# A transformer layer at its two stage boundaries: the squares for the second normalisation written to a PSUM bank, in four pieces

## The chip, the core and the metric

The kernel runs on one core of one Trainium2 chip. A core has a matrix engine (TensorE, PE in the profile, with its weight loads shown apart as PEld), a vector engine (VectorE, DVE), a scalar engine (ScalarE, ACT), a small general engine (GpSimd, POOL) and an engine that issues most of the transfers (SyncE, SP). They run side by side and wait for each other through semaphores. Data lies in SBUF; the matrix engine writes its results to PSUM, a second memory of eight banks, each 512 fp32 numbers wide on all 128 partitions. The metric is the device time of one execution in microseconds (us).

## What is computed

One layer over 256 tokens of width D = 2048, in fp32: a gated feed-forward block, a token mixer (attention and an mLSTM) and a second feed-forward block. Between the blocks stands the piece that the change touches: the residual sum goes through a layer norm with learned gain and bias, and its result through a second layer norm, without parameters, whose output is scaled and shifted by vectors made from the condition `c`.

```python
def _modulate(x, shift, scale):
    return _layernorm(x) * (1 + scale) + shift

def _layer(...):
    h = _swiglu(_modulate(x, sh1, sc1), ffn1_w_in, ffn1_w_out)
    x = _layernorm(ALPHA * x + 0.5 * (1 + g1) * h, ln1_g, ln1_b)
    h = _token_mixer(_modulate(x, sh2, sc2), w_in, ...)
    x = _layernorm(ALPHA * x + (1 + g2) * h, ln2_g, ln2_b)
    h = _swiglu(_modulate(x, sh3, sc3), ffn2_w_in, ffn2_w_out)
    return _layernorm(ALPHA * x + 0.5 * (1 + g3) * h, ln3_g, ln3_b)
```

## The kernel before

Every fp32 product is made of three matmuls on rounded parts (`mm3`, lines 368 to 370: high times high, high times low, low times high). Weights arrive in 1 MB pieces (`raw`), ACT rounds each to its high part (line 142) and DVE takes the difference as the low part (line 143). Beside this stream DVE builds the conditioning vectors (`acc`, line 157, from `ar`). The 256 tokens are two halves of 128, called a = 0 and a = 1 below; `res` holds both.

`out_proj` ends a block: its last 512 columns are multiplied for a = 0 and then for a = 1 (`products(0)`, `products(1)`), into one PSUM tile each (`o_f` after the first feed-forward block, `o_mx` after the mixer). Then `boundary` runs, once after the first feed-forward block (at 769 us of the trace, the **first boundary**) and once after the mixer (at 1173 us, the **second boundary**). For each half it

- adds the product to the residual and takes its statistics (`add_up`, lines 432 to 437; `row_std`, 258 to 260, with the power on POOL at line 248 in `rsqrt`);
- runs the layer norm over `res` in two passes (`ln_affine`): line 485 subtracts the mean and multiplies by the gain, line 490 scales, adds the bias and gives the row sum of each piece (pieces of 1024, 512 and 512 columns);
- has ACT square each piece after a shift (line 495), of which only the row sum is used. The squares themselves are never read: they go to an SBUF tile `sq` in the pool `np2` or `np3`;
- makes mean and reciprocal deviation of the second normalisation from these sums in a row of DVE operations on single columns (`ln_stats`, lines 501 to 518);
- normalises 256 columns at a time (`n`: the first tile on DVE at line 310, the others on ACT at 312), transposes them on PE (`tp`, line 316), scales and shifts (`xf`, ACT 326 and DVE 323), and splits the result in high and low part (`xhi`, 332; `xlo`, 333).

PE takes up the first tiles of the next stage directly from `xf`, in single fp32 matmuls against the first three weight pieces (`cols_1024`, line 618: `mo` at the first boundary, `ge` at the second): all of a = 0, then all of a = 1.

The order on DVE inside `boundary` is the order of the code (`manual_schedule`); on the other engines a scheduler sets it. SBUF pools lie on a stack at the two ends of the memory: a tile of a new pool may lie where a pool just released had tiles, and its first writer then waits for their last reader. At the second boundary `np3` takes the room of `mx`, the mixer's pool, of which the tiles `yh` and `yl` are read by products of `products(1)`. PSUM has a pool of five banks for accumulators (`mm_tile`), given out in the order in which they come free, and one of three for the rest (`aux_tile`).

## Time and profile before

| | us |
|---|---|
| median of three runs | 1939.93 |
| lowest and highest of them | 1935.54, 1943.65 |
| the profiled execution | 1937.79 |
| its span in the trace | 1936.1 |
| PE busy in the span | 1895.1 |
| DVE busy | 1474.7 |
| ACT busy | 944.7 |

The profiled execution took 1937.79 us, of which the trace covers 1936.1; the other 1.7 lie around it. Times in the rows below count from the start of the span. A row of the timeline gives the start, the duration, the engine, the line, the operation with its output and inputs, and in brackets how long the engine had been idle and who ended that. The granted clock (PEclk) is the share of its full clock that TensorE was given.

### The profile page before, as it was taken

To read this page: it belongs to the slowest core of one execution; us is meant where nothing else is said; L and a number is where in the kernel's file an instruction comes from. 1 tells how busy PE (TensorE), PEld (TensorE's weight loads), DVE (VectorE), ACT (ScalarE), POOL (GpSimd) and SP (SyncE) were. 2 spreads that over 40 slices of the span, in tenths; PEclk is the share of its full clock that TensorE was granted. 3 is DMA by queue.
4 is the path that set the end of the run, shared out by engine and by line. 5 is a ranking of instruction groups with operands and counts; after the bars stand their busy time and mean duration, and the time that the engine had idled before them with its cause. 6 is when DMAs were issued, how large, how long until landed. Compare 5 with 4: busy or idle time off the path is not lost.

```text
span 1936.1 us, 32201 instructions
## 1 busy us (share of the span) xinstructions
PE 1895.1 (98%) x13069; PEld 1717.0 (89%) x13069; DVE 1474.7 (76%) x1818; ACT 944.7 (49%) x1336; POOL 56.4 (3%) x82
## 2 busy tenths in 40 slices
PE   6999999999999999999999999999999999999997
PEld 3999999999978887699999785998999999988886
DVE  6788988776889898688988787767766665555776
ACT  3554454443454554745755534555444444444552
POOL 1111100000000000000000000000000000000000
PEclk9999999999999999999999999999999999999999
DMA  9978869899898886499889783987776775655552
GB/s 357 378 261 313 324 229 310 299 315 303 278 343 304 284 302 219 142 317 305 291 293 306 276 298 140 309 294 251 253 253 226 261 238 196 239 184 188 194 195 87
DMA packets 295693, 510.90 MB, mean 264 GB/s; under 512 B 10834, under 2 KB 158706, under 8 KB 294520
## 3 DMA queue, kind: packets, MB, share of 16 engines
q1 hardware_dynamic: 287768, 480.53, 72.8%
q0 software_dynamic: 7776, 28.32, 4.1%
q8 instruction: 102, 1.67, 0.3%
q14 instruction: 47, 0.39, 0.1%
HBM read 506.71 MB, written 2.10 MB: 263 GB/s over the span
## 4 chain that ended last, share of the span: by engine, by line
PE 75%; issue 11%; DMA 6%; DVE 5%; ACT 2%; POOL 0%; SPq 0%; DVEq 0%; ACTq 0%; POOLq 0%
PE gu_f L369 8%; PE gu_f L370 8%; PE gu_f L368 8%; PE o_f L368 7%; PE o_f L370 7%; PE o_f L369 7%; PE s L369 5%; PE s L368 5%; PE s L370 5%; DMA ar<-in_w_ada_dram 3%; PE fh L368 2%; PE fh L370 2%; PE fh L369 1%; PE fs L370 1%; PE fs L369 1%
## 5 line engine op out<-in xcount | busy, mean ns | idle before, releaser
L157 DVE SCALAR_TENSOR_TENSOR acc<-ar,csil,acc 128x1024 f32<-128x1024 f32 x242 | 307.8, 1272 | 84.4 <-DMA ar<-in_w_ada_dram 83.2
L369 PE MATMUL s<-xlo_f,hi_s 128*128 128x256 f32 x768 | 213.4, 278 | 1.6 <-DVE xlo_f L300 1.6
L368 PE MATMUL s<-xhi_f,hi_s 128*128 128x256 f32 x768 | 213.4, 279 | 0.0
L370 PE MATMUL s<-xhi_f,lo_s 128*128 128x256 f32 x768 | 213.2, 278 | 0.0
L370 PE MATMUL gu_f<-xhi_f,lo_f2i 128*128 128x256 f32 x768 | 212.0, 276 | 0.0
L368 PE MATMUL gu_f<-xhi_f,hi_f2i 128*128 128x256 f32 x768 | 212.0, 276 | 0.0
L369 PE MATMUL gu_f<-xlo_f,hi_f2i 128*128 128x256 f32 x768 | 212.0, 276 | 0.0
L143 DVE TENSOR_TENSOR lo_f2i<-raw_f2i,hi_f2i 128x1024 fp32r<-128x1024 f32 x96 | 117.6, 1225 | 89.2 <-ACT hi_f2i L142 89.2
L370 PE MATMUL gu_f<-xhi_f,lo_f1i 128*128 128x256 f32 x640 | 176.7, 276 | 0.0
L368 PE MATMUL gu_f<-xhi_f,hi_f1i 128*128 128x256 f32 x640 | 176.7, 276 | 0.0
L369 PE MATMUL gu_f<-xlo_f,hi_f1i 128*128 128x256 f32 x640 | 176.7, 276 | 0.0
L142 ACT CAST hi_f2i<-raw_f2i 128x1024 fp32r<-128x1024 f32 x96 | 100.8, 1050 | 135.2 <-PE gu_f L369 124.3
L142 ACT CAST hi_s<-raw_s 128x1024 fp32r<-128x1024 f32 x96 | 100.4, 1051 | 130.4 <-PE s L369 87.5
L369 PEld LDWEIGHTS s<-xlo_f,hi_s 128*128 128x128 f32 x768 | 145.3, 189 | 1.9 <-DVE xlo_f L300 1.9
L370 PEld LDWEIGHTS s<-xhi_f,lo_s 128*128 128x128 f32 x768 | 145.2, 189 | 0.0
L368 PEld LDWEIGHTS s<-xhi_f,hi_s 128*128 128x128 f32 x768 | 145.0, 189 | 0.0
L368 PEld LDWEIGHTS gu_f<-xhi_f,hi_f2i 128*128 128x128 f32 x768 | 144.2, 188 | 0.2
L369 PEld LDWEIGHTS gu_f<-xlo_f,hi_f2i 128*128 128x128 f32 x768 | 144.2, 188 | 0.2
L370 PEld LDWEIGHTS gu_f<-xhi_f,lo_f2i 128*128 128x128 f32 x768 | 144.2, 188 | 0.0
L143 DVE TENSOR_TENSOR lo_f2o<-raw_f2o,hi_f2o 128x1024 fp32r<-128x1024 f32 x88 | 107.7, 1224 | 44.9 <-ACT hi_f2o L142 44.8
L143 DVE TENSOR_TENSOR lo_s<-raw_s,hi_s 128x1024 fp32r<-128x1024 f32 x96 | 115.9, 1221 | 29.6 <-ACT hi_s L142 29.5
L368 PE MATMUL o_f<-hi_f2o,hh 128*128 128x512 f32 x344 | 135.2, 393 | 0.0
(485 smaller groups left out, 5344.9 us busy)
## 6 DMA issues: line engine op xcount, KB each, us to landing
ar<-in_w_ada_dram SPq DMA_DIRECT2D x227, 512.0 KB, 5.3
raw_f2i<-in_ffn_w_in_dram SPq DMA_DIRECT2D x48, 1024.0 KB, 5.1
raw_s<-in_ffn_w_in_dram SPq DMA_DIRECT2D x47, 1024.0 KB, 7.7
raw_f1o<-in_ffn_w_out_dram SPq DMA_DIRECT2D x44, 1024.0 KB, 7.3
raw_f2o<-in_ffn_w_out_dram SPq DMA_DIRECT2D x44, 1024.0 KB, 5.1
raw_f1i<-in_ffn_w_in_dram SPq DMA_DIRECT2D x40, 1024.0 KB, 7.5
ar<-in_w_ada_dram POOLq DMA_DIRECT2D x48, 512.0 KB, 6.9
raw_mxo<-in_w_out_dram SPq DMA_DIRECT2D x16, 1024.0 KB, 6.7
```

The source lines that it names most:

```text
L142: S.copy(hi, src)
L143: return V.tensor_tensor(out=lo, in0=src, in1=hi.bitcast(F32), op=ALU.subtract)
L157: V.scalar_tensor_tensor(out=acc, in0=raw, scalar=csil[:, k:k + 1], in1=acc, op0=ALU.mult, op1=ALU.add)
L368: PE.matmul(o, ah, bh, start=start, stop=False)
L369: PE.matmul(o, ah, bl, start=False, stop=False)
L370: PE.matmul(o, al, bh, start=False, stop=stop)
```

## The change

The tile `sq` of SBUF goes. Each boundary takes one accumulator bank of PSUM (`mm_tile`) for the squares of both halves, all pieces on top of each other. A bank is 512 numbers wide, so the second pass of the layer norm and the squares are cut into four pieces of 512 columns instead of 1024, 512, 512. The shift of the squares is the mean of the first piece, now of 512 columns (factor -4/D for -2/D), and `ln_stats` is adapted: one more row sum to add to the mean, one more sum of squares (a DVE operation more, ahead of the first `yield 1`), and the difference of mean and shift is taken from the mean itself. In `boundary` the DVE order stays: the first of the pieces of a = 1 stands where it stood, the rest where the last two stood.

```diff
-        for i, (c0, c1) in enumerate(((0, 1024), (1024, 1536), (1536, 2048))):
-            r = res[:, a, c0:c1]
-            V.scalar_tensor_tensor(out=r, in0=r, scalar=rs, in1=lgb[1][:, c0:c1], op0=ALU.mult, op1=ALU.add,
-                                   accum_out=sums[:, i:i + 1])
+        for i in range(4):
+            cs = slice(i * 512, (i + 1) * 512)
+            r = res[:, a, cs]
+            total, squares = ((k, k + 1) for k in ((0, 1, 2, 6)[i], (5, 7, 8, 9)[i]))
+            V.scalar_tensor_tensor(out=r, in0=r, scalar=rs, in1=lgb[1][:, cs], op0=ALU.mult, op1=ALU.add,
+                                   accum_out=sums[:, slice(*total)])
             if i == 0:
-                V.tensor_scalar_mul(sums[:, 4:5], sums[:, 0:1], -2.0 / D)
-            sq = npool.tile([P, 1024], F32, tag="sq", name=f"sq_{tag}{a}{i}")
-            S.activation(sq[:, :c1 - c0], r, AF.Square, bias=sums[:, 4:5], accum_out=sums[:, 7 + i:8 + i])
+                V.tensor_scalar_mul(sums[:, 4:5], sums[:, 0:1], -4.0 / D)
+            S.activation(sq, r, AF.Square, bias=sums[:, 4:5], accum_out=sums[:, slice(*squares)])
             yield
 
     def ln_stats(out_, sums):
         s = [sums[:, i:i + 1] for i in range(10)]
-        V.tensor_tensor(out=s[1], in0=s[1], in1=s[2], op=ALU.add)
+        V.tensor_scalar(out=s[1], in0=s[1], scalar1=s[2], scalar2=s[6], op0=ALU.add, op1=ALU.add)
...
-        V.tensor_scalar(out=s[3], in0=s[1], scalar1=s[0], scalar2=1.0 / D, op0=ALU.subtract, op1=ALU.mult)
+        V.tensor_tensor(out=s[3], in0=mean, in1=s[4], op=ALU.subtract)
         yield
         V.tensor_scalar(out=s[2], in0=s[3], scalar1=s[3], scalar2=-1.0, op0=ALU.mult, op1=ALU.mult)
         yield
         V.tensor_scalar_add(s[2], s[2], EPS)
+        yield
+        V.tensor_tensor(out=s[7], in0=s[7], in1=s[5], op=ALU.add)
         yield 1
...
+        sq = mm_tile(f"sq_{tag}")
         with tc.manual_schedule(engines={mybir.EngineType.DVE}):
...
-            aff = [ln_affine(a, rs[a], mv[a], lgb, sums[a], tag) for a in range(2)]
+            aff = [ln_affine(a, rs[a], mv[a], lgb, sums[a], sq) for a in range(2)]
...
             next(aff[1])
             next(m0[2])
-            next(aff[1])
-            next(aff[1])
+            for _ in aff[1]:
+                pass
             together(lns[1])
```

On ACT, at the second boundary, for a = 0 (`hi_mxo` is the last weight piece of the mixer's projection; the brackets name the engines whose semaphores the instruction waits for). Before:

```order
L142 COPY hi_mxo_01_12275<-raw_mxo_0_12269 128x1024 [waits PE_49,Activation_49]
L495 ACTIVATE sq_12416,sums_12399<-res,sums_12399 128x1024 [waits DVE_49,PE_49,Pool_49]
L495 ACTIVATE sq_12419,sums_12399<-res,sums_12399 128x512 [waits DVE_49,Activation_49]
L495 ACTIVATE sq_12422,sums_12399<-res,sums_12399 128x512 [waits DVE_49,Activation_49]
L312 ACTIVATE n_12439<-res,mr_12401 128x256 [waits DVE_49,Pool_49]
L326 ACTIVATE xf_12451<-tp_12435,scsh 128x128 [waits PE_49]
```

And with the change:

```order
L142 COPY hi_mxo_01_12276<-raw_mxo_0_12270 128x1024 [waits PE_49,Activation_49]
L496 ACTIVATE sq_12404,sums_12400<-res,sums_12400 128x512 [waits DVE_49]
L496 ACTIVATE sq_12404,sums_12400<-res,sums_12400 128x512 [waits DVE_49,Activation_49] x3
L312 ACTIVATE n_12441<-res,mr_12402 128x256 [waits DVE_49,PE_49,Pool_49]
L326 ACTIVATE xf_12453<-tp_12437,scsh 128x128 [waits PE_49]
```

The first square no longer waits for PE; the wait for PE, which belongs to the memory that `np3` takes over, has moved on to the first writers of `n`.

On DVE, at the second boundary, the second pass and the statistics of a = 1 (`mr` holds what `ln_stats` gives). Before:

```order
L490 TENSOR_SCALAR res,sums_12400<-res,rs_12398,lb_11668 128x1024
L493 TENSOR_SCALAR sums_12400<-sums_12400 128x1
L490 TENSOR_SCALAR res,sums_12400<-res,rs_12398,lb_11668 128x512 x2
L501 TENSOR_TENSOR sums_12400<-sums_12400 128x1
L504 TENSOR_SCALAR mr_12402<-sums_12400 128x1
L506 TENSOR_SCALAR sums_12400<-sums_12400 128x1
L508 TENSOR_SCALAR sums_12400<-sums_12400 128x1
L510 TENSOR_SCALAR sums_12400<-sums_12400 128x1
L333 TENSOR_TENSOR xlo_f_12385<-xf_12451,xhi_f_12384 128x2x128
L333 TENSOR_TENSOR xlo_f_12385<-xf_12461,xhi_f_12384 128x2x128
L512 TENSOR_SCALAR sums_12400<-sums_12400 128x1
```

And with the change:

```order
L492 TENSOR_SCALAR res,sums_12401<-res,rs_12399,lb_11669 128x512
L495 TENSOR_SCALAR sums_12401<-sums_12401 128x1
L492 TENSOR_SCALAR res,sums_12401<-res,rs_12399,lb_11669 128x512 x3
L502 TENSOR_SCALAR sums_12401<-sums_12401 128x1
L505 TENSOR_SCALAR mr_12403<-sums_12401 128x1
L507 TENSOR_TENSOR sums_12401<-mr_12403,sums_12401 128x1
L509 TENSOR_SCALAR sums_12401<-sums_12401 128x1
L511 TENSOR_SCALAR sums_12401<-sums_12401 128x1
L513 TENSOR_TENSOR sums_12401<-sums_12401 128x1
L333 TENSOR_TENSOR xlo_f_12386<-xf_12453,xhi_f_12385 128x2x128
L333 TENSOR_TENSOR xlo_f_12386<-xf_12463,xhi_f_12385 128x2x128
L515 TENSOR_SCALAR sums_12401<-sums_12401 128x1
```

The sum of the first two squares (line 513) is new and stands ahead of the two `xlo` differences, so that the rest of the statistics of a = 1 (from line 512 before, 515 now) comes behind one operation more.

On PE, at the second boundary, where the matmuls of a = 0 (`ge_12561`, with the change `ge_12563`) end and the transposes of a = 1 begin. Before:

```order
L618 MATMUL ge_12561<-raw_gu_12392,xf_12468 128x512
L618 MATMUL ge_12560<-raw_gu_12392,xf_12468 128x512
L316 MATMUL tp_12493<-ident,n_12491 128x128 x2
L316 MATMUL tp_12498<-ident,n_12496 128x128 x2
L618 MATMUL ge_12561<-raw_gu_12392,xf_12468 128x512
L316 MATMUL tp_12506<-ident,n_12504 128x128 x2
L618 MATMUL ge_12562<-raw_gu_12386,xf_12501 128x512
L316 MATMUL tp_12517<-ident,n_12515 128x128 x2
L618 MATMUL ge_12563<-raw_gu_12386,xf_12501 128x512
L316 MATMUL tp_12522<-ident,n_12520 128x128 x2
```

And with the change:

```order
L622 MATMUL ge_12562<-raw_gu_12393,xf_12469 128x512
L622 MATMUL ge_12563<-raw_gu_12393,xf_12469 128x512
L316 MATMUL tp_12495<-ident,n_12493 128x128 x2
L316 MATMUL tp_12500<-ident,n_12498 128x128 x2
L622 MATMUL ge_12564<-raw_gu_12387,xf_12503 128x512
L316 MATMUL tp_12508<-ident,n_12506 128x128 x2
L622 MATMUL ge_12565<-raw_gu_12387,xf_12503 128x512
L316 MATMUL tp_12519<-ident,n_12517 128x128 x2
L316 MATMUL tp_12524<-ident,n_12522 128x128 x2
```

One matmul of a = 0 (two in the profile's count, since an fp32 matmul shows there as two) has moved ahead of the first transposes of a = 1. At the first boundary the order on PE is the same as before, and apart from the places shown no instruction of the program has another place on PE, ACT or DVE, but for one cast of a = 1 on ACT at the second boundary; POOL and SP have the order that they had.

More of the change, by code (lines that the diff above doesn't have):

```diff
@@ L477, in ln_params, with ln_affine @@
         return lg, lb
-    def ln_affine(a, rs, mv, lgb, sums, tag):
+    def ln_affine(a, rs, mv, lgb, sums, sq):
         for h in range(2):
```

## The prediction

> **What bounds the kernel now.** I read the page's first part, the waits of PE, the clock by stretches, and then the timeline at the two boundaries, since the change touches nothing else. From the page, then the waits of PE (whole span, then from 1200 us on; total, times, longest), then stretches with PE's busy time first and the granted clock third from the end, and one row of PE's timeline:

> ```profile
> PE 1895.1 (98%) x13069; PEld 1717.0 (89%) x13069; DVE 1474.7 (76%) x1818; ACT 944.7 (49%) x1336; POOL 56.4 (3%) x82
> ...
> PE tp L316 <- DVE n L310: 2.2, 2, 2.0
> ...
> PE bc L170 <- ACT ahi L142: 0.4, 1, 0.4
> ...
> 1065.80 0.33 PE L1058 MATMUL ptp<-ident,s 128*128 128x128 f32 x1 [1.65 <-ACT s L1053]
> ...
> 1066.00:1076.00 10.00, 10.00 (x49) 8.14 (x49) 8.07 (x11) 5.21 (x11) 0.00 (x0) 1.00 0.85 284
> 1181.00:1186.00 5.00, 3.06 (x14) 2.17 (x12) 1.63 (x9) 2.88 (x6) 0.54 (x1) 1.00 0.00 0
> 1186.00:1191.00 5.00, 4.65 (x11) 2.11 (x12) 4.86 (x9) 4.08 (x11) 2.10 (x2) 0.66 0.27 105
> ```

> PE is busy 98% of the span, so only what shortens PE's own idle time or its slow stretches can show at the end. One of its waits is at a boundary: 2.0 us for the first normalised tile. And something follows it: in the five us behind it the clock is 0.66 on average, so 5 x (1 - 0.66) = 1.7 us of PE work are lost there as well. A gap of 1.65 us at 1065.80 was followed by ten us at full clock. From 1200 us to the end PE waits for an instruction in all 0.4 us: whatever PE gains at the second boundary has nothing behind it that would take it back.

> The second boundary in order of time (a = 0 to the first transposes, then the end of a = 1):

> ```profile
> 1177.94 1.28 DVE L490 SCALAR_TENSOR_TENSOR res<-res,rs,lb 128x1024 f32<-128x1024 f32 x1
> ...
> 1179.26 0.15 DVE L493 TENSOR_SCALAR sums<-sums 128x1 f32<-128x1 f32 x1
> ...
> 1180.92 0.39 PE L370 MATMUL o_mx<-hi_mxo,yl 128*128 128x512 f32 x1
> ...
> 1181.12 0.21 DVE L506 TENSOR_SCALAR sums<-sums 128x1 f32<-128x1 f32 x1
> ...
> 1181.36 0.21 DVE L508 TENSOR_SCALAR sums<-sums 128x1 f32<-128x1 f32 x1
> ...
> 1181.39 1.15 ACT L495 ACTIVATE sq<-res,sums 128x1024 f32<-128x1024 f32 x1 [12.37 <-DVE sums L506]
> ...
> 1183.52 0.72 ACT L495 ACTIVATE sq<-res,sums 128x512 f32<-128x512 f32 x1
> 1183.66 0.40 PE L370 MATMUL o_mx<-hi_mxo,ylo 128*128 128x512 f32 x1
> ...
> 1184.37 0.27 DVE L512 TENSOR_SCALAR sums<-sums 128x1 f32<-128x1 f32 x1 [2.60 <-ACT sq L495]
> ...
> 1185.55 0.41 DVE L310 TENSOR_SCALAR n<-res,mr 128x256 f32<-128x256 f32 x1 [0.66 <-POOL mr L248]
> ...
> 1185.95 0.69 DVE L432 TENSOR_TENSOR o_mx<-o_mx,gate 128x512 f32<-128x512 f32 x1
> 1186.02 0.44 PE L316 MATMUL tp<-ident,n 128*128 128x128 f32 x2 [1.96 <-DVE n L310]
> ...
> 1195.36 0.27 DVE L512 TENSOR_SCALAR sums<-sums 128x1 f32<-128x1 f32 x1
> ...
> 1198.59 0.60 PE L316 MATMUL tp<-ident,n 128*128 128x128 f32 x4
> ...
> 1201.03 0.60 ACT L312 ACTIVATE n<-res,mr 128x256 f32<-128x256 f32 x1
> ...
> 1202.44 8.75 PE L618 MATMUL ge<-raw_gu,xf 128*128 128x512 f32 x20
> ```

> The shift of the squares is ready at 1179.41 (line 493), yet ACT, idle, starts the first square at 1181.39. What it waited for is the last product that reads `yl`, which ends at 1180.92 + 0.39 = 1181.31: `sq` lies in memory of the mixer's pool. The bracket names line 506, which ends at 1181.33, by coincidence. From the first square on everything is a chain: squares, line 512, POOL, line 310, transpose. The last product on PE ended at 1184.06, so PE stood for 1.96 us.

> The first boundary, where `sq` met no such reader (a = 0, then a = 1), and three groups of ACT by form with their mean in ns:

> ```profile
> 774.96 0.15 DVE L493 TENSOR_SCALAR sums<-sums 128x1 f32<-128x1 f32 x1
> 775.03 0.74 DVE L490 SCALAR_TENSOR_TENSOR res<-res,rs,lb 128x512 f32<-128x512 f32 x1
> ...
> 775.23 1.15 ACT L495 ACTIVATE sq<-res,sums 128x1024 f32<-128x1024 f32 x1 [17.94 <-DVE sums L493]
> ...
> 775.70 0.75 DVE L490 SCALAR_TENSOR_TENSOR res<-res,rs,lb 128x512 f32<-128x512 f32 x1
> ...
> 776.51 0.72 ACT L495 ACTIVATE sq<-res,sums 128x512 f32<-128x512 f32 x1
> ...
> 777.36 0.72 ACT L495 ACTIVATE sq<-res,sums 128x512 f32<-128x512 f32 x1
> ...
> 778.20 0.27 DVE L512 TENSOR_SCALAR sums<-sums 128x1 f32<-128x1 f32 x1 [0.74 <-ACT sq L495]
> ...
> 779.28 0.40 PE L370 MATMUL o_f<-hi_f1o,hl 128*128 128x512 f32 x1
> ...
> 779.86 0.44 PE L316 MATMUL tp<-ident,n 128*128 128x128 f32 x2 [0.19 <-DVE n L310]
> ...
> 788.45 0.75 DVE L333 TENSOR_TENSOR xlo_mx<-xf,xhi_mx 128x256 fp32r<-128x256 f32 x2
> ...
> 789.20 0.27 DVE L512 TENSOR_SCALAR sums<-sums 128x1 f32<-128x1 f32 x1
> ...
> 791.23 0.14 PEld L316 LDWEIGHTS tp<-ident,n 128*128 128x128 f32 x1 [0.31 <-ACT n L312]
> 791.59 0.60 PE L316 MATMUL tp<-ident,n 128*128 128x128 f32 x4
> ...
> L495 ACT ACTIVATE sq<-res,sums 128x512 f32<-128x512 f32 x8 | 5.8, 722 | 0.3
> ...
> L495 ACT ACTIVATE sq<-res,sums 128x1024 f32<-128x1024 f32 x4 | 4.6, 1152 | 33.8 <-DVE sums L493 21.4 <-DVE sums L506 12.4
> ...
> L1188 ACT ACTIVATE nps<-yM 128x256 f32<-128x256 f32 x8 | 3.1, 387 | 0.1
> ```

> Here the square starts 0.27 after line 493, and PE stands only 0.19 us. It is the picture that the second boundary should take on.

> **The change, part by part.** Prices first. A DVE piece of 512 instead of 1024 makes the first piece 1.28 - 0.74 = 0.54 shorter; a fourth piece adds 0.67 (775.03 to 775.70): the second pass is 0.13 longer in all, while its first sum comes 0.54 earlier. The new single-column sum costs 0.24 (1181.12 to 1181.36). A square of 512 columns follows the one before it by 0.85 (776.51 to 777.36) into SBUF. Into PSUM the trace has no square of 512, but the mLSTM's square of 256 (line 1188): 387 ns; into SBUF 256 would take 722 - (1152 - 722)/2 = 507. So the PSUM piece lies between no cheaper (0.85 apart) and 0.12 cheaper (0.73 apart). I take the second, since line 1188 is the same function into the same memory; both are kept below.

> Second boundary, a = 0. Line 493's counterpart moves to 1179.26 - 0.54 = 1178.72, the first square to 1178.99, nothing of PE being awaited. The fourth starts at 1178.99 + 3 x 0.73 = 1181.18 (or 1181.54), and line 512's counterpart can follow 0.84 later (777.36 to 778.20), at 1182.0 (1182.4). DVE itself reaches it at 1181.36 + 0.24 (line 510) + 0.13 + 0.24 (new sum) + 0.24 = 1182.2. So 1182.2 to 1182.4 in place of 1184.37; line 310 is 1.18 behind (1183.4 to 1183.6), the transposes 0.47 behind that: 1183.9 to 1184.05. `n` now inherits the wait for `yl`, but that ends at 1181.31, two us ahead of it. PE is on its products till 1184.06. So the transposes start at about 1184.1: **1.9 us of idle time go**, and what ends last there is PE itself.

> The slow clock. With no gap there is no reason left in this trace for the drop: at the first boundary, with a gap of 0.19, the stretch from the transposes of a = 0 to those of a = 1 took 791.59 - 779.86 = 11.73. At the second it took 1198.59 - 1186.02 = 12.57 with two matmuls fewer; these are now ahead of the transposes and cost 8.75/20 = 0.44 each. 12.57 + 0.87 - 1.70 = 11.74: the two stages agree once the slow clock is taken out. So PE could be at the transposes of a = 1 at 1184.1 + 11.7 = 1195.8.

> But a = 1 has to be ready. DVE's line 432 waits for PE's last product (1184.06), so it moves from 1185.95 to 1184.1, by 1.85 and not by more. From there the chain of a = 1 carries the longer pass and the new sum ahead of the `xlo` differences, 0.13 + 0.24 = 0.37; line 512 goes from 1195.36 to 1193.9. The weight load of the transposes is 2.03 behind it (789.20 to 791.23) and takes 0.14: they start at 1196.1. PE waits some 0.3 us for them. That is 2.5 earlier than 1198.59. Of the 0.87 moved ahead not all is kept, since ACT makes the next `n` at its own pace: the third of them ends 3.04 behind the transposes (1201.63 - 1198.59), so at 1199.1, and the long run of 20 matmuls starts at about 1199.6 instead of 1202.44. **Gain of PE at the second boundary: 2.8**, between 2.5 and 3.3.

> First boundary. For a = 0 the squares were not late: line 512 goes from 778.20 to 777.9 (DVE bound) or 778.1, the transposes from 779.86 to 779.6 or 779.75: a gain of 0.1 to 0.25. For a = 1 DVE is what ends last: `xlo` ends at 789.20 and line 512 stands right behind it. There the 0.37 counts, less some 0.07 by which DVE starts earlier: 789.5. The weight load at 791.23 was already waiting for `n`; it goes to about 791.5, the transposes from 791.59 to 791.7, and ACT's next tiles come 0.3 later. **A loss of 0.1 to 0.3; I take 0.2.** Between the boundaries PE has gaps of its own (the 1.65 above), so part may vanish.

> The PSUM bank costs nothing by the order in which banks come free: `ge` and `mo` of a = 0 get banks whose readers ended before the transposes start, and those of a = 1 get the banks of the last two products, emptied by lines 432 and 434 within 1.5 us of line 432's start, ten us ahead of their use. Without that cover a `mo` matmul would wait for line 434, about 1.4 us at each boundary. The SBUF shift at the first boundary (`n` and `xf` 4 KB lower) changes waits only for readers that ended ten us earlier.

> Sum: -2.8 + 0.2 = **-2.6 us**. The profiled execution took 1937.79 with a span of 1936.1, so 1935.2 and 1933.5. It lies 2.1 below the median of the runs shown; against the median, 1939.93, I forecast **1937.3 us**.

> **The rivals.** *The slow clock stays.* The trace has one gap followed by slow matmuls at a boundary; it does not prove that the gap made them slow. Then the transposes of a = 1 come at 1184.1 + 11.73 + 1.70 = 1197.5, with the two matmuls done: the gain is 1198.59 + 0.87 - 1197.5 = 1.9, and with the first boundary 1.7: 1938.2. For it: a gap of 1.65 did nothing, 1.96 is hardly more. Against it: no other drop stands in the middle of the kernel. [...] Chance 0.13.

> *The square did not wait for memory but for line 506, as the bracket says.* Then it still starts behind it, at 1181.39 + 0.13, and with four squares line 512 comes at 1181.52 + 3 x 0.73 + 0.84 = 1184.55, later than now, nothing is saved, and with 0.2 at the first boundary and 0.4 here the time is 1940.5. Against: at the first boundary the same instruction ran at 775.23, before the last DVE piece had started, and line 506 comes behind that piece. Chance 0.05.

> *Slower: the longer DVE chain of a = 1 opens a new gap, and the clock drops at it.* Place: the transposes of a = 1 at both boundaries, where PE comes earlier and `n` later. Price: the gap itself, and 1.7 when it is long enough. It decides from a gap between 1.65 (no drop) and 1.96 (drop); my rows give 0.1 to 0.3. If the pieces cost so much more that the gap reaches 1.8, the first boundary loses 1.8 + 1.7 = 3.5, and the second, with its gap of 2.0 back at another place, gains nothing: 1943.4. Chance 0.06.

> **How the numbers follow.** The forecast has 0.70, the three rivals 0.13, 0.05 and 0.06; 0.06 is left for what I do not see, such as another PSUM bank order that costs later. A measurement of this kernel tells about 0.5%, 9.7 us, from no change. All cases lie within that, so the same has 0.91. The three runs of before are 8.1 us apart, and a median of three may fall that far off: faster 0.06, slower 0.03. The mechanism alone spans -3.6 to +0.6 around the median, 1936.3 to 1940.5; with two to four us for the scatter of a median the range is 1932.5 to 1942.5, which also holds the rivals but the slower one.

> **What would show it.** The first square of a = 0 at the second boundary starts about 0.3 behind its shift; the wait of PE for line 310 falls from 2.0 to below 0.3; the granted clock in the five us behind is 1.00; squares of 512 take about 0.60; the transposes of a = 1 there follow those of a = 0 by about 12.0, with PE waiting below 0.5 for `n`; at the first boundary those of a = 1 come 0.1 to 0.3 later. I am wrong if PE still stands a microsecond or more at either boundary, if the clock still drops there, or if the time moves by more than 5 us.

## The result, and the profile after

| | before | after |
|---|---|---|
| median, us (22 runs of each) | 1938.87 | 1935.65 |
| lowest and highest | 1933.30, 1944.25 | 1933.09, 1940.03 |
| the profiled execution | 1937.79 | 1933.09 |
| its span | 1936.1 | 1931.4 |

The ratio is 0.9984, with a 95% interval of 0.9976 to 0.9992: 3.1 us less, between 1.6 and 4.7. The forecast was 2.6 less and 1937.3 us, within 0.5% of before. Among the runs below, one of before (2332 us) and one of e2 (4938 us) were far slower than the rest; the ratios leave them out.

The busy times on the page of the changed kernel:

```profile
PE 1893.5 (98%) x13069; PEld 1716.8 (89%) x13069; DVE 1476.1 (76%) x1830; ACT 947.0 (49%) x1344; POOL 56.4 (3%) x82
```

PE's waits between 1170 and 1211 us in it, of which there is one (total, times, longest):

```profile
PE tp L316 <- ACT n L312: 0.3, 1, 0.3
```

And the two stretches of its second boundary (PE's busy time first, the granted clock third from the end):

```profile
1181.00:1186.00 5.00, 4.66 (x20) 2.66 (x19) 3.94 (x10) 3.18 (x10) 1.50 (x3) 1.00 0.12 48
1186.00:1191.00 5.00, 5.00 (x13) 2.22 (x12) 4.93 (x12) 3.11 (x9) 1.14 (x1) 1.00 0.14 57
```

The wait of 2.0 us for line 310 is gone. The clock, 0.66 on average in the five us behind the gap before, is 1.00. The 0.3 us that is left is a wait for the second `n` tile, and it was there before too.

The timeline of the second boundary after the change (the square is now line 496, the last line of the sums 515), then two rows of the first boundary:

```profile
1177.53 0.15 DVE L495 TENSOR_SCALAR sums<-sums 128x1 f32<-128x1 f32 x1
1177.72 0.69 ACT L496 ACTIVATE sq<-res,sums 128x512 f32<-128x512 f32 x1 [9.11 <-DVE sums L495]
...
1178.57 0.69 ACT L496 ACTIVATE sq<-res,sums 128x512 f32<-128x512 f32 x1
...
1179.42 0.69 ACT L496 ACTIVATE sq<-res,sums 128x512 f32<-128x512 f32 x1
...
1180.26 0.69 ACT L496 ACTIVATE sq<-res,sums 128x512 f32<-128x512 f32 x1
...
1181.11 0.28 DVE L515 TENSOR_SCALAR sums<-sums 128x1 f32<-128x1 f32 x1 [0.16 <-ACT sq L496]
...
1182.46 0.40 PE L370 MATMUL o_mx<-hi_mxo,ylo 128*128 128x512 f32 x1
...
1182.77 0.44 PE L316 MATMUL tp<-ident,n 128*128 128x128 f32 x2
...
1187.84 0.75 DVE L492 SCALAR_TENSOR_TENSOR res<-res,rs,lb 128x512 f32<-128x512 f32 x1
...
1192.63 0.27 DVE L515 TENSOR_SCALAR sums<-sums 128x1 f32<-128x1 f32 x1
...
1194.66 0.93 PE L316 MATMUL tp<-ident,n 128*128 128x128 f32 x4
...
1206.49 0.80 PE L368 MATMUL ge<-hi_gu,xhi_f 128*128 128x512 f32 x1
...
776.25 0.40 PE L370 MATMUL o_f<-hi_f1o,hl 128*128 128x512 f32 x1
776.64 0.44 PE L316 MATMUL tp<-ident,n 128*128 128x128 f32 x2
```

The square starts 0.19 behind its shift (1177.53 to 1177.72; 2.13 before), while PE is still on its products, and the transposes follow the last product with nothing between them, at both boundaries. To compare spans of one place in different executions I cut each boundary at four marks on PE's timeline: the start of the last product, of a = 0's first transpose, of a = 1's first transpose, and of the first matmul with split weights of the next stage (`ge<-hi_gu` at 1206.49; before, 1210.63). All in us:

| | before | after | difference |
|---|---|---|---|
| up to the last product of the first boundary | 779.28 | 776.25 | -3.03 |
| first boundary | 24.74 | 24.69 | -0.05 |
| between the boundaries | 379.64 | 381.52 | +1.88 |
| second: product to transposes of a = 0 | 2.36 | 0.31 | -2.05 |
| second: a = 0 to a = 1 | 12.57 | 11.89 | -0.68 |
| second: a = 1 to split weights | 12.04 | 11.83 | -0.21 |
| second boundary, sum | 26.97 | 24.03 | -2.94 |
| from there to the end of the span | 725.47 | 724.91 | -0.56 |

The sum is -4.7, the difference of the two spans. Two of its large terms lie where the programs are the same: up to the first boundary, and between the boundaries. Between the boundaries four profiles of before alone range from 379.64 to 392.01, and the nine of the other kernels (below) from 378.99 to 386.07. That scatter is larger than the effect, and so the effect has to be read at the boundaries.

### The profile page after: what moved, and what is told of

Read it like the earlier page. It is cut to its first block, busy times and chain, and to the rows that moved or that the text cites. A ratio compares the mean times of both kernels' runs of the same rounds, so it can differ in the third digit from the quotient of the medians.

```text
span 1931.4 us, 32227 instructions
## 1 busy us (share of the span) xinstructions
PE 1893.5 (98%) x13069; PEld 1716.8 (89%) x13069; DVE 1476.1 (76%) x1830; ACT 947.0 (49%) x1344; POOL 56.4 (3%) x82
## 4 chain that ended last, share of the span: by engine, by line
PE 82%; issue 10%; DMA 4%; DVE 2%; ACT 1%; POOL 0%; SPq 0%; DVEq 0%; ACTq 0%; POOLq 0%
PE gu_f L370 8%; PE gu_f L369 8%; PE gu_f L368 8%; PE o_f L368 8%; PE o_f L370 8%; PE o_f L369 8%; PE s L369 5%; PE s L368 5%; PE s L370 5%; PE o_mx L370 2%; PE fh L370 2%; PE fh L369 2%; PE fh L368 2%; PE o_mx L369 1%; PE o_mx L368 1%
## 5 line engine op out<-in xcount | busy, mean ns | idle before, releaser
L370 PE MATMUL s<-xhi_f,lo_s 128*128 128x256 f32 x768 | 213.4, 278 | 0.0
L370 PE MATMUL gu_f<-xhi_f,lo_f2i 128*128 128x256 f32 x768 | 212.0, 276 | 0.0
L370 PE MATMUL gu_f<-xhi_f,lo_f1i 128*128 128x256 f32 x640 | 176.7, 276 | 0.0
L142 ACT CAST hi_f2i<-raw_f2i 128x1024 fp32r<-128x1024 f32 x96 | 100.8, 1050 | 135.2 <-PE gu_f L369 124.3
L142 ACT CAST hi_s<-raw_s 128x1024 fp32r<-128x1024 f32 x96 | 100.6, 1052 | 130.1 <-PE s L369 94.6
L370 PEld LDWEIGHTS s<-xhi_f,lo_s 128*128 128x128 f32 x768 | 145.3, 189 | 0.0
L370 PEld LDWEIGHTS gu_f<-xhi_f,lo_f2i 128*128 128x128 f32 x768 | 144.2, 188 | 0.0
```

What stands on the lines that cost most here:

```text
L142: S.copy(hi, src)
L370: PE.matmul(o, al, bh, start=False, stop=stop)
```

## The experiments

The kernels e0, e3, e4, e5 and e10 are before and after once more, for what their profiles show at the same place. The others change one thing. All rows are measured with the marks of the last table (gap = idle time of PE ahead of a = 0's transposes; drop = a stretch at half clock behind it):

| | first boundary | gap at the second | drop | a = 0 to a = 1 | second boundary |
|---|---|---|---|---|---|
| before | 24.74 | 1.96 | yes | 12.57 | 26.97 |
| e0, before | 24.74 | 1.96 | no | 11.37 | 25.92 |
| e4, before | 24.74 | 1.96 | yes | 12.57 | 26.97 |
| e5, before | 24.74 | 1.97 | no | 11.37 | 25.93 |
| after | 24.69 | none | no | 11.89 | 24.03 |
| e3, after | 24.68 | none | no | 11.89 | 24.03 |
| e10, after | 24.69 | none | no | 11.90 | 24.03 |
| e1, four pieces, `sq` in the old place | 24.69 | 2.38 | yes | 12.56 | 27.38 |
| e2, four pieces, `sq` in a place of its own | 24.69 | none | no | 11.89 | 24.03 |
| e6, after, six additions late | 24.69 | 1.04 | no | 11.68 | 25.22 |
| e7, after, twelve additions late | 24.68 | 2.18 | no | 11.69 | 26.35 |
| e8, new form for a = 0 alone | 24.57 | none | no | 11.76 | 23.83 |
| e9, the same | 24.57 | none | no | 11.75 | 23.83 |

Within one kernel, with the same clock behind the gap, the boundaries repeat to 0.03 us, against some ten us between runs as a whole.

**e0: before once more, for the clock behind its gap.**

> The kernel before once more, for the scatter of its stages. The second boundary, from the start of the last product on PE to the first matmul with a split weight (ge<-hi_gu), took 26.97 us and should again take 26.8 to 27.2, with PE's wait of about 2.0 for line 310 and a granted clock near 0.66 in the five us behind it. If the drop of the clock comes by chance and not from the gap, it may be missing here, and the stage takes 25.3. The first boundary should take 24.7. The stretches outside the boundaries may differ by up to 3 us from the first profile.

The gap came back to the hundredth, and the drop did not; the stage took 25.92, where I had set 25.3 without one. PE's timeline of this run:

```profile
1182.22 0.40 PE L370 MATMUL o_mx<-hi_mxo,ylo 128*128 128x512 f32 x1
...
1184.58 0.44 PE L316 MATMUL tp<-ident,n 128*128 128x128 f32 x2 [1.96 <-DVE n L310]
...
1195.95 0.93 PE L316 MATMUL tp<-ident,n 128*128 128x128 f32 x4 [0.34 <-ACT n L312]
```

The stretch behind its gap (clock third from the end):

```profile
1184.58:1190.08 5.50, 5.17 (x16) 2.57 (x17) 5.36 (x9) 4.09 (x11) 2.10 (x2) 1.00 0.24 95
```

The same stretch of the first profile of before, whole and by single microseconds:

```profile
1186.02:1191.52 5.50, 5.17 (x12) 2.36 (x13) 5.36 (x9) 4.18 (x11) 2.10 (x2) 0.69 0.25 95
...
1186.00:1187.00 1.00, 0.65 (x4) 0.40 (x4) 0.97 (x3) 0.87 (x3) 0.06 (x1) 1.00 0.00 0
1187.00:1188.00 1.00, 1.00 (x4) 0.33 (x3) 0.96 (x2) 1.00 (x4) 0.52 (x1) 0.72 0.00 0
1188.00:1189.00 1.00, 1.00 (x4) 0.42 (x3) 0.93 (x4) 0.61 (x2) 0.34 (x1) 0.50 0.47 172
1189.00:1190.00 1.00, 1.00 (x3) 0.49 (x2) 1.00 (x2) 0.61 (x2) 1.00 (x1) 0.50 0.81 315
1190.00:1191.00 1.00, 1.00 (x3) 0.47 (x2) 1.00 (x2) 1.00 (x4) 0.19 (x1) 0.57 0.09 37
```

The drop is a clock of 0.50 from 1187.44 to 1190.86, for 3.4 us; it begins 1.4 us behind the end of the gap (1186.02) and loses 0.28 + 0.50 + 0.50 + 0.43 = 1.7 us of work. In e0, without it, PE issued sixteen matmuls in these 5.50 us, and not twelve. But of the 1.7 us only 1.05 show in the stage (26.97 - 25.92): PE at full clock then waits 0.34 for a = 1's `n`, which it did not when slow, and the stretch after that is 0.15 longer (12.19 for 12.04). These two make up 0.49 of the missing 0.65; the rest is open. The one time of this run was 1934.78.

**e1: the four pieces with `sq` in SBUF, in the pool where it lay before.**

```diff
-        sq = mm_tile(f"sq_{tag}")
+        sq = npool.tile([P, 1024], F32, tag="sq", name=f"sq_{tag}")[:, :512]
```

> The change with its four pieces, but the squares go to SBUF as before (a tile in the pool that takes the mixer's room). My theory, that the square waits for PE's last reader of the mixer's pool: the first square of a = 0 at the second boundary still starts 0.08 behind the last product that reads yl, the four squares take 4 x 0.85 from there, 0.4 longer than the three before, PE's gap is 2.4, the clock drops again, and the stage takes 27.2 to 27.5; time by 0.0 to 0.5 us longer than before. The rival that the wait is for the column sums (line 506 before, 507 here): the square starts right behind line 507, whatever PE does. The rival that the four pieces themselves gain: the stage is below 26.5.

The timeline of e1:

```profile
1183.75 0.16 DVE L495 TENSOR_SCALAR sums<-sums 128x1 f32<-128x1 f32 x1
...
1185.94 0.39 PE L370 MATMUL o_mx<-hi_mxo,yl 128*128 128x512 f32 x1
...
1186.41 0.72 ACT L496 ACTIVATE sq<-res,sums 128x512 f32<-128x512 f32 x1 [11.58 <-PE o_mx L370]
1186.51 0.16 DVE L507 TENSOR_TENSOR sums<-mr,sums 128x1 f32<-128x1 f32 x1
...
1191.46 0.44 PE L316 MATMUL tp<-ident,n 128*128 128x128 f32 x2 [2.38 <-DVE n L310]
```

The stretch behind its gap:

```profile
1191.46:1196.96 5.50, 5.17 (x12) 2.43 (x13) 5.36 (x9) 4.18 (x11) 2.10 (x2) 0.69 0.30 95
```

The shift is ready at 1183.91, and the square starts at 1186.41: 0.08 behind the end of the last product that reads `yl` (1185.94 + 0.39 = 1186.33), and 0.10 ahead of line 507, which stands where before the row named in the bracket stood. The bracket now says PE. So the wait was for PE's last reader of that memory, and not for the sums; e2 is the other half of the proof. The four pieces alone make the second boundary 0.41 longer (27.38 for 26.97, both with a drop), since a fourth square follows behind the wait. Over 12 runs the median was 1942.43, the ratio 1.0009 [0.9997, 1.0021], not to be told from no change.

**e2: as e1, with the squares of the second boundary at a place of their own.** The room is taken from a new pool before the products and given back after the boundary; the squares are written in bfloat16 there, and their row sums are made as before.

```diff
+        if tag == "2":
+            sq = ent["sq"].tile([P, 512], mybir.dt.bfloat16, name="sq_far")
...
+        ent["sq"] = tc.alloc_tile_pool(name="sqp", bufs=1)
...
+    ent["sq"].release()
```

> As the run with four pieces in SBUF, but at the second boundary the squares go to a small SBUF tile in room that the mixer's pool never had (in bfloat16, so that it fits; their row sums are as before). My theory, that only the wait for memory counts and PSUM has no part in it: the first square starts about 0.3 behind its shift, PE has no gap above 0.2 ahead of its first transposes, the clock stays at 1.00, and the second boundary takes 24.0 as with the change; time about 3 us below before. The rival that PSUM as the target makes the gain (shorter squares, no SBUF write beside other engines): the stage stays at 25 or more, with squares spaced by more than the 0.85 of the changed kernel.

The timeline of e2:

```profile
1185.56 0.15 DVE L495 TENSOR_SCALAR sums<-sums 128x1 f32<-128x1 f32 x1
1185.74 0.72 ACT L496 ACTIVATE sq_far<-res,sums 128x512 bf16<-128x512 f32 x1 [9.16 <-DVE sums L495]
...
1186.59 0.72 ACT L496 ACTIVATE sq_far<-res,sums 128x512 bf16<-128x512 f32 x1
...
1190.48 0.40 PE L370 MATMUL o_mx<-hi_mxo,ylo 128*128 128x512 f32 x1
...
1190.79 0.44 PE L316 MATMUL tp<-ident,n 128*128 128x128 f32 x2
```

The squares are in SBUF and take 0.72, 0.85 apart, and yet the boundary is 24.03, as in the changed kernel. PSUM has no part of its own in the gain; it is one way to be rid of the pool that must first come free. No run has three pieces without the wait at this boundary, so what the cut into four is worth to a = 0 is not separated there; at the first boundary, where the squares of before never met the wait, three pieces left a gap of 0.19, so an estimate for it is about 0.2. Median 1937.57 of 12 runs, ratio 0.9987 [0.9972, 1.0001].

**e3: after once more.**

> The changed kernel once more, beside the others on the same chip. Second boundary 23.9 to 24.2, first 24.6 to 24.8, no wait of PE above 0.5 at either, clock 1.00 throughout; time 2 to 4 us below before. If the stretch between the boundaries is again 1.9 us longer than in the first profile of before, part of the gain is given back there; if it differs the other way, that was scatter.

The stages are those of the first profile to 0.01. The ratio was 0.9991 [0.9979, 1.0003] (1937.59, 12 runs; before beside it 1939.33). The stretch between the boundaries was 386.07, with 381.52 in the first profile of the same kernel: it is scatter, and no part of the gain is seen to be given back there.

**e4 and e5: before twice more.** e0 had left the clock as a matter of chance or of something that differs between runs.

> The kernel before a third time. In its first profile PE's gap of 1.96 at the second boundary was followed by a half clock, in the second profile the same gap of 1.96 was not. [...] Then the stage takes 25.9 without a drop or 27.0 with one, nothing between, and the gap is 1.96 again. The rival that something else lengthens the stage (a transfer, another engine): the gap or the stage has a third value.

> The kernel before a fourth time: 25.9 without a drop of the clock or 27.0 with one, gap 1.96; of four profiles I expect one to three with a drop.

The stretch behind the gap in e4, clock third from the end:

```profile
1195.45:1200.95 5.50, 5.17 (x12) 2.51 (x13) 5.36 (x9) 4.19 (x11) 2.11 (x2) 0.69 0.31 95
```

In e5 the same stretch, and one behind another gap:

```profile
1197.01:1202.51 5.50, 5.18 (x16) 2.56 (x17) 5.36 (x9) 4.09 (x11) 2.10 (x2) 1.00 0.29 95
...
1035.29:1040.79 5.50, 5.50 (x30) 5.27 (x31) 3.96 (x8) 2.55 (x8) 0.00 (x0) 0.69 0.75 251
```

That other gap on PE's timeline of e5:

```profile
1035.29 0.55 PE L1058 MATMUL ptp<-ident,s 128*128 128x128 f32 x3 [1.55 <-DVE gate L211]
```

A drop in e4, none in e5: two of four for the same gap of 1.96 or 1.97. And in e5 a gap of 1.55 elsewhere was followed by one (a clock of 0.69 over 5.50 us).

```profile
1184.03:1187.44 3.41, 1.12 (x6) 0.70 (x6) 2.31 (x7) 1.61 (x6) 1.04 (x2) 1.00 0.00 0
...
1193.78:1197.19 3.41, 1.42 (x6) 0.70 (x6) 2.63 (x7) 1.63 (x4) 1.12 (x2) 1.00 0.00 0
...
1180.65:1184.06 3.41, 1.97 (x9) 1.29 (x7) 0.49 (x2) 2.18 (x6) 0.52 (x1) 1.00 0.00 0
1184.06:1187.47 3.41, 2.56 (x10) 1.41 (x11) 3.22 (x8) 2.78 (x8) 0.84 (x3) 1.00 0.08 32
...
1193.28:1196.69 3.41, 1.76 (x8) 1.12 (x6) 0.64 (x3) 1.97 (x6) 0.54 (x1) 1.00 0.00 0
1196.69:1200.10 3.41, 2.77 (x10) 1.43 (x11) 3.27 (x8) 2.99 (x8) 1.03 (x2) 1.00 0.23 88
```

In before the stretch holds the whole gap, in e4 all but 0.29 us of it and PE's next short wait: PE is busy for only 1.12 and 1.42 us, and the clock drops. In e0 and e5 a mark cuts the gap further on, each stretch keeps 1.76 us or more of work, and the clock does not drop. The last section counts this over all profiles.

The single times of e4 and e5, 1946.64 and 1947.16, with 1942.79 for before beside them, say how little one run tells here.

**e6 and e7: a gap put back by late additions.** Six or twelve additions of zero on a single column are put behind the last sum of a = 0 at the second boundary of the changed kernel.

```diff
+        for _ in range(extra):
+            V.tensor_scalar_add(s[6], s[6], 0.0)
...
-            lns = [ln_stats(mr[a], sums[a]) for a in range(2)]
+            lns = [ln_stats(mr[a], sums[a], 6 if tag == "2" and a == 0 else 0) for a in range(2)]
```

> The changed kernel with six more single-column additions of 0 on DVE in the statistics of a = 0 at the second boundary, some 0.25 us each, so that the first normalised tile comes 1.5 us later. Theory: PE's gap ahead of the transposes becomes 1.4 to 1.5 and the stage 25.4 to 25.6 without a drop of the clock (gaps of 1.5 had none in most cases so far), 26.5 with one. The rival that the gap itself is harmless, since a = 1 or a transfer is what ends last: the stage stays below 24.6.

> The same with twelve additions: a gap of 2.9 to 3.0. Theory: long enough for a drop wherever it falls (all gaps from 2.4 us on had one so far), so the granted clock is 0.50 for some 3.4 us behind it, and the stage takes 27.9 to 28.2. The rival that a drop at this place is chance whatever the length: full clock, and a stage of 26.9 to 27.0.

The timeline of e7:

```profile
1181.32 2.23 DVE L519 TENSOR_SCALAR sums<-sums 128x1 f32<-128x1 f32 x12
...
1184.69 0.44 PE L316 MATMUL tp<-ident,n 128*128 128x128 f32 x2 [2.18 <-DVE n L310]
```

The stretch behind its gap:

```profile
1184.69:1190.19 5.50, 5.16 (x16) 2.56 (x17) 5.36 (x9) 4.09 (x11) 2.11 (x2) 1.00 0.29 95
```

An addition costs 2.23/12 = 0.19, less than I had set, so the gaps came out at 1.04 and 2.18. They pass into the stage whole or more: 25.22 - 24.03 = 1.19 and 2.32. So e7 did not reach the 2.9 that its theory was about; for the clock these runs tell only that the gaps of 1.04 and 2.18 were followed by none. One run of each, 1940.5 and 1935.11.

**e8 and e9: the new form for a = 0 alone.** a = 1 keeps its three pieces and its `sq` in SBUF.

```diff
-            aff = [ln_affine(a, rs[a], mv[a], lgb, sums[a], tag) for a in range(2)]
-            lns = [ln_stats(mr[a], sums[a]) for a in range(2)]
+            aff = [ln_affine(a, rs[a], mv[a], lgb, sums[a], tag, None if a else bank) for a in range(2)]
+            lns = [ln_stats(mr[a], sums[a], a == 0) for a in range(2)]
```

> The change for a = 0 alone, at both boundaries: its squares in four pieces to the PSUM bank, while a = 1 keeps the three pieces and the SBUF tile of before (its first square has no reader of the mixer's pool left to wait for). My theory, that all of the gain sits in a = 0 of the second boundary and that the longer chain of a = 1 costs only some 0.1 us: no gap above 0.1 ahead of the transposes of a = 0, clock 1.00, the second boundary takes 23.9 to 24.0 (24.03 with the whole change), the first 24.55 to 24.65 (24.69); time 2 to 3 us below before, not to be told from the whole change. The rival that a = 1 gains from PSUM too: the second boundary takes 24.3 or more.

> The change for a = 0 alone once more, timed beside the whole change on the same chip. By the stages it should be 0.3 us shorter than the whole change (24.57 and 23.83 against 24.69 and 24.03), far below what the runs can tell: both 2 to 3 us below before, their medians within 2 us of each other. If it is again 2 us or more ahead of the whole change, something outside the two boundaries differs between them.

The boundaries are 24.57 and 23.83 in both (I had set 23.9 to 24.0 for the second): 0.12 and 0.20 less than with the whole change. That is what the change costs a = 1, whose squares never met the wait. The times cannot tell 0.3 us: e8 gave 0.9971 [0.9961, 0.9982], and e9, the same kernel, 0.9993 [0.9977, 1.0009]; the median of e9, 1939.30, is 2.3 above that of the whole change beside it (e10), more than the 2 that I had set and against the order of the stages. In e8 stands the longest gap without a drop, on PE's timeline:

```profile
1066.00 0.33 PE L1080 MATMUL ptp<-ident,s 128*128 128x128 f32 x1 [2.75 <-ACT s L1075]
```

The stretch behind it, at full clock (third from the end):

```profile
1066.00:1071.50 5.50, 5.50 (x25) 4.34 (x26) 4.92 (x6) 3.34 (x6) 0.00 (x0) 1.00 0.71 209
```

**e10: after a third time.**

> The whole change beside it: stages 24.69 and 24.03 again, 2 to 3 us below before, within 2 us of the run with a = 0 alone.

The stages again, and 0.9987 [0.9970, 1.0003]. The whole change measured three times is -3.1, -1.7 and -2.5 us; only the first of the three intervals excludes no change.

## Why the prediction was right, step by step

**The memory wait, and its removal: right.** e1 brings the wait back with the old place of `sq`, and e2 takes it away without PSUM. In e1 the first writer in the new pool started 0.08 behind the last reader of the pool that it replaced, and in e2, at a place of its own, 0.18 behind its shift (1185.56 to 1185.74). The 1.9 us of idle time are gone (1.96 before, none after), and PE's own products end last, as forecast.

**The price of a square into PSUM: the wrong end was chosen.** I took 0.73 from one to the next and about 0.60 for the square itself; it was 0.85 and 0.69. The group of ACT by form in the changed kernel, 692 ns for 722 in SBUF, then one readout of the row sum after and one before (line 495, first boundary):

```profile
L496 ACT ACTIVATE sq<-res,sums 128x512 f32<-128x512 f32 x16 | 11.1, 692 | 29.2 <-DVE sums L495 28.8
L496 ACT ACTIVATION_READ_ACCUMULATOR sq<-res,sums 128x1 f32 x16 | 3.0, 187 | 0.0
...
1178.35 0.19 ACT L496 ACTIVATION_READ_ACCUMULATOR sq<-res,sums 128x1 f32 x1
...
777.14 0.19 ACT L495 ACTIVATION_READ_ACCUMULATOR sq<-res,sums 128x1 f32 x1
```

The square itself is 30 ns shorter and not 120, but squares still follow each other by 0.85 (1177.72, 1178.57, 1179.42). In both kernels the readout starts 0.63 behind the start of its square (1177.72 to 1178.35; 776.51 to 777.14), and the next square 0.22 behind that: the end that came earlier was not what the next one waited for. The comparison with line 1188 took a difference of durations for one of spacing; why even that difference was not 120 ns at 512 columns is open. It did not show at the end: line 515 came at 1181.11, bound by ACT, and the first `n` was ready before PE's last product ended.

**The slow clock: a sure term that is a chance.** The step that failed is "with no gap there is no reason left for the drop" as a full 1.7 us in the sum. The half of it that speaks of the changed kernel held: without a gap none of the six profiles (after, e2, e3, e8, e9, e10) has a drop at this boundary. But before had it in two profiles of four, at the same gap: in the two in which PE was busy for only 1.12 and 1.42 us between two marks 3.41 us apart. So on these four it is worth half; and of the 1.7 us lost, 1.05 reach the next stage. The gain at the second boundary is therefore 2.94 against a profile with a drop and 25.92 - 24.03 = 1.89 against one without, 2.4 on the mean of the four. My 2.8 was right for the one profile that I had, and about 0.4 too much for the runs.

**The rival "the slow clock stays"** fell: the clock is 1.00 at 1186 to 1191. **The rival that line 506 was awaited** fell by e1. **The slower rival** did not come: no new wait of PE shows at either boundary. The limit that it used, "between 1.65 (no drop) and 1.96 (drop)", fell too, as a drop followed 1.55 (and 1.10, in e4 at 240.01), and once or more none followed 1.96, 2.18 and 2.75: the length of the gap alone does not tell them apart.

**The chain of a = 1: right in place, a little large.** From the first piece of the second pass to the last sum it took 4.48 before (1190.88 to 1195.36) and takes 1192.63 - 1187.84 = 4.79: 0.31 more, where I set 0.37. The transposes stand 11.89 behind those of a = 0, for 12.0; in e8, where this part is undone, 11.76. So they are some 0.13 late and not 0.3, and the trace names no wait of PE for it.

**The first boundary: the sign was wrong.** I set a loss of 0.2; it gained 0.05. The gain for a = 0 was of the size expected (0.19, the whole gap). For a = 1 the last sum came 0.25 later, about as set: 10.17 behind the start of the last product (776.25 to 786.42), for 9.92 before. So did the weight load of the transposes, 12.20 for 11.95:

```profile
788.45 0.20 PEld L316 LDWEIGHTS tp<-ident,n 128*128 128x128 f32 x2 [0.72 <-ACT n L312]
```

But the transposes now start with that load, and not 0.2 behind it as I had set; before, they stood 0.36 behind it (791.23 to 791.59), since PE was still on its matmuls. So they come 0.11 earlier against the last product (12.20 for 12.31), and ACT's next tile of `n`, which I had 0.3 later, comes 0.05 earlier (13.04 for 13.09). Counted from a = 0's transposes, those of a = 1 are 0.08 later, and what follows 0.06, together less than a = 0 gained. e8 has the part of a = 1 by itself: 0.12.

**The PSUM bank costs nothing: right.** In the changed kernel no matmul waits for a bank at either boundary: one wait of 0.3 for `n` is the only one at each.

The sum of the measured terms is -0.05 - 1.89 to -0.05 - 2.94, that is -1.9 to -3.0, and the three measured ratios give -1.7 to -3.1. The forecast of -2.6 lies within both. That it came so close owes something to two errors that cancel: the clock 0.4 too much, the first boundary 0.25 too little. And the time alone, with its interval of 1.6 to 4.7, could not have told a right sum from these; the stages do.

## What to carry to other kernels

An engine that starts late though its inputs are ready may wait for the room it writes to. Here a new pool lay on the place of an old one, its first square started 0.08 behind the old one's last reader, and the profile of before named a neighbour that ended 0.02 us later (1181.33 for 1181.31). Move such a throw-away output to any memory that is free early, and keep the finer cut to the half that gains from it: for a = 1 it cost 0.12 and 0.20 us here. A slow stretch seen behind a gap in one profile may be a chance and not a price, as here, where a drop followed the gap of 1.96 in two of four profiles of one kernel: take more profiles before it enters a sum, and compare stages that repeat to hundredths where whole runs scatter by ten microseconds.

## What the runs showed of the hardware

**Equal gaps, unequal clocks.** Over the 13 profiles, PE's gaps outside the first 50 us and the stretches behind them give this count:

| gap, us | with a drop | of |
|---|---|---|
| 0.9 to 1.5 | 1 | 36 |
| 1.5 to 2.3 | 7 | 30 |
| 2.38 and more | 7 | 8 |

The middle class reaches from a drop at 1.55 to none at 2.24. The eighth of the last class is the 2.75 in e8. The length alone does not sort them. PE's busy time between two marks, 3.41 us apart and placed by the recorded changes of the clock of each execution, sorts them better (stretches from 50 us to 15 us before the end, without those that are themselves slow):

| PE busy between two marks, us | followed by a drop | of |
|---|---|---|
| up to 1.44 | 11 | 11 |
| 1.53 to 1.66 | 3 | 7 |
| 1.73 and more | 1 | 7084 |

The one in the last row, in e4 ahead of 241.46, holds the gap of 1.10 and eight matmuls of a single column, which show as 1.19 us of busy time. The 2.75 in e8 lies across two such stretches, with PE busy for 2.06 and 2.01 us of them. A gap of 1.96 that lies whole between two marks leaves at most 1.45 us for work; if the marks may fall anywhere against it, this happens in (3.41 - 1.96)/3.41 = 0.43 of the executions, an estimate from these numbers, beside the two of four seen (in one of them the gap was not quite whole). The table is a count over these 13 profiles; what makes the clock drop, and why its changes lie 3.413 us apart, is not shown.

**Shorter squares, the same spacing.** Of 512 columns with a row sum, a square took 692 ns into PSUM and 722 into SBUF, and ACT's rate stayed at one in 0.85 us, with the readout of the sum 0.63 behind the start of the square in both.
